# Second SwiGLU block: feature pairs without the norm's factor, and two direct tiles in place of four

## The chip, the cores and the metric

The kernel runs on one core of one Trainium2 chip. A core has engines that each work through their own list of instructions: TensorE (PE, matrix products), VectorE (DVE), ScalarE (ACT), GpSimd (POOL) and SyncE (SP, which here only issues transfers). They wait for one another by semaphores. The metric is the device time of one execution in microseconds (us), from start to end.

## The reference

One decoder layer, float32, on x of 512 tokens by 1024 features:

```python
x = x + 0.5 * swiglu(rms_norm(x, g_ffn1), w_ffn1_gate, w_ffn1_up, w_ffn1_down)
h = rms_norm(x, g_mix)
# three groups of heads (windowed attention, convolution, cross-attention to 256 memory tokens)
x = x + concat(y_attn, y_conv, y_mem) @ w_out
x = x + 0.5 * swiglu(rms_norm(x, g_ffn2), w_ffn2_gate, w_ffn2_up, w_ffn2_down)

def swiglu(x, w_gate, w_up, w_down):
    return (jax.nn.silu(x @ w_gate) * (x @ w_up)) @ w_down

def rms_norm(x, g):
    return x * lax.rsqrt(jnp.mean(x * x, axis=-1, keepdims=True) + EPS) * g
```

The hidden width is 2816, 22 tiles of 128. The two SwiGLU blocks have the same shapes; the change is in the second.

## The kernel before

x lies transposed: 8 feature tiles of 128 partitions by 512 tokens (`x[:, d]`). Every float32 operand is split in a high part, rounded to the type that PE multiplies (`whi`, `xh`, `hh`, `bh`), and the rest (`wlo`, `xl`, `hl`, `bl`), and a product is three matmuls: high x high, high x rest, rest x high. ACT makes the high part (line 167 for weights), DVE the rest (line 168).

**The norm's factor.** The gain is multiplied into `xh` and `xl` (`scaled_split`, lines 358 and 359). The factor of a token, `rb`, is a number for each token and so commutes with the product over features. It is made late: the squares of all feature tiles are summed (`sqsum`, line 373), `Norm.stats` sums them over partitions on PE (line 378) and takes the reciprocal root on DVE in small steps (lines 332 to 337), then broadcasts it (line 383); `Norm.spread` transposes that on PE (`tp<-ident,t`, line 391) and copies it to `rb` (line 392).

**The tiles of a SwiGLU block.** A tile f of the hidden width is made in one of two ways.

- *Direct* (f < `N_DIRECT` = 4): `mm3` multiplies gate and up by `xh` and `xl`, 24 matmuls of 512 columns each (lines 347 to 349). `evac` multiplies both results by `rb` (lines 410 and 413), with the silu on ACT and their product on DVE (line 414).
- *Fast* (the others): gate and up over two halves of the features, and x over two halves of the features and of the tokens, are a 2 x 2 by 2 x 2 block product with seven block products in place of eight (`fast` and `product`, lines 444 to 446), 12 matmuls of 256 columns each, 84 in all. It needs sums of weights (`make_sums`, lines 126 to 129: `s` of four 512-column adds) and combinations of x. `blocks(k)` makes the latter for the feature tiles k and k + 4, with the factor `rb` in them, one k after each direct tile: `braw` (21, 22, 11, 12; line 423, twice), `bmade` (T3, Q1, Q2, T4; lines 432 to 434) and their split `bh`, `bl` (seven blocks of 256; lines 436 and 437).

The T4 product of tile f takes a weight split of its own (`vhi`, `vlo`, 512 columns, one buffer each) and writes to a bank of the tag `sc`; the other products write to `mm` banks, of which there are four.

**The down product** runs in six rounds over hidden tiles 0-3, 4-7, 8-11, 12-15, 16-17 and 18-21 (`ROUNDS`); `steps(f)` says which pieces stand within which tile: the first three pieces of round 0 ahead of tile 4, the fourth in tile 5, then one in each tile from 8. A round's result is scaled by 0.5 and added to x: on DVE (line 506), but for the first two pieces of round 0 by ACT (line 502) and an accumulating transfer of POOL (line 503). The result is stored as the last round makes it.

**What sets the order.** Transfers of weights are issued on SP ahead of use (`W.load_to`), splits three items ahead (`W.next`). Within that a scheduler fixes each engine's list when the program is built; numbers in the names below follow the order in which the code was written, so that the rows show how far an engine's list leaves it. Each tag of a pool has a number of buffers (`sum` 3, `kept` 3, `t` 5, `mm` 4, `sc` and `tp` 2), and a new tile waits for the buffer's last reader.

## Time and profile before

| | us |
|---|---|
| three runs | 869.84, 865.34, 865.73 |
| median | 865.73 |
| profiled execution, its own time | 870.17 |
| span of the profile, first to last instruction | 868.1 |
| PE busy in it | 861.3 |
| DVE busy | 698.3 |
| ACT busy | 446.0 |
| POOL busy | 27.9 |

The profiled execution is near the slowest of the three runs, and 2.07 us of its time lie outside the span. A row of the timeline gives the start, the duration, engine, line, operation, the output and the inputs by name; in brackets stands how long the engine was idle before it and which instruction it waited for. In the order of time the second block takes: tiles 0 and 1 from 529.20 to 551.16, tiles 2 and 3 to 573.14, the first pieces of the down product to 589.94, the fast tiles from there to the last product at 864.9.

### The profile page before, as it was taken

How to read it: one execution, taken by the hardware profiler on the slowest of the kernel's cores; microseconds unless marked ns; L12 is line 12 of the kernel's file. 1: busy time of each engine (PE TensorE's matmuls, PEld its weight loads, DVE VectorE, ACT ScalarE, POOL GpSimd, SP SyncE). 2: the span in 40 equal slices, each digit the busy share in tenths (PEclk: the TensorE clock that was granted, in tenths of full speed). 3: DMA queues.
4: the chain of work that ended last, by engine and by line, in shares of the span. 5: the costliest groups of instructions: out<-in, count | busy, mean ns of one | idle time of the engine just before them, and what ended most of it. 6: DMA issues, size and time to landing. Idle time of an engine off the chain costs nothing.

```text
span 868.1 us, 15720 instructions
## 1 busy us (share of the span) xinstructions
PE 861.3 (99%) x6361; PEld 795.1 (92%) x6361; DVE 698.3 (80%) x1163; ACT 446.0 (51%) x740; POOL 27.9 (3%) x30
## 2 busy tenths in 40 slices
PE   9999999999999999999999999999999999999998
PEld 5889999999999999988776878889999999999998
DVE  7998877777868887869989976997987878787772
ACT  7455545455554454632939754454554444545440
POOL 0010000000000000300000021010000000000000
PEclk9999999999999999999999999999999999999999
DMA  7326334334454344232020333336333333333312
GB/s 271 122 83 165 94 97 122 99 110 134 111 145 146 97 113 130 95 97 62 0 62 13 110 89 84 99 90 159 105 106 121 95 121 85 116 98 99 121 49 99
DMA packets 34809, 91.45 MB, mean 105 GB/s; under 512 B 3248, under 2 KB 5808, under 8 KB 34736
## 3 DMA queue, kind: packets, MB, share of 16 engines
q1 hardware_dynamic: 32000, 85.99, 32.1%
q0 software_dynamic: 1584, 2.88, 2.1%
q10 hardware_dynamic: 1152, 1.57, 0.7%
q8 instruction: 50, 0.82, 0.4%
q14 instruction: 23, 0.19, 0.1%
HBM read 85.45 MB, written 2.10 MB: 101 GB/s over the span
## 4 chain that ended last, share of the span: by engine, by line
PE 92%; DVE 3%; ACT 2%; issue 1%; DMA 1%; SPq 0%; ACTq 0%; DVEq 0%
PE mm L347 15%; PE mm L348 14%; PE mm L349 14%; PE mm L444 11%; PE mm L446 11%; PE mm L445 11%; PE sc L444 2%; PE sc L446 2%; PE sc L445 2%; PE sc L347 1%; PE sc L349 1%; PE sc L348 1%; PE tp L948 1%; PE tp L962 1%; ACT p L913 1%
## 5 line engine op out<-in xcount | busy, mean ns | idle before, releaser
L444 PE MATMUL mm<-bh,whi 128*128 128x256 f32 x864 | 239.9, 278 | 0.2 <-ACT kept L459 0.2
L446 PE MATMUL mm<-bh,wlo 128*128 128x256 f32 x864 | 239.6, 277 | 0.0
L445 PE MATMUL mm<-bl,whi 128*128 128x256 f32 x864 | 239.6, 277 | 0.0
L348 PE MATMUL mm<-hl,whi 128*128 128x256 f32 (+1 forms) x640 | 184.7, 289 | 0.0
L349 PE MATMUL mm<-hh,wlo 128*128 128x256 f32 (+1 forms) x640 | 184.6, 289 | 0.0
L347 PE MATMUL mm<-hh,whi 128*128 128x256 f32 (+1 forms) x640 | 184.1, 289 | 0.0
L167 ACT CAST whi<-wraw 128x1024 fp32r<-128x1024 f32 (+2 forms) x122 | 124.1, 1021 | 106.2 <-PE mm L348 45.0
L168 DVE TENSOR_TENSOR wlo<-wraw,whi 128x1024 fp32r<-128x1024 f32 (+2 forms) x122 | 145.4, 1193 | 34.4 <-ACT whi L167 34.0
L446 PEld LDWEIGHTS mm<-bh,wlo 128*128 128x128 f32 x864 | 163.1, 189 | 0.0
L444 PEld LDWEIGHTS mm<-bh,whi 128*128 128x128 f32 x864 | 162.2, 188 | 0.5 <-ACT kept L459 0.4
L445 PEld LDWEIGHTS mm<-bl,whi 128*128 128x128 f32 x864 | 162.2, 188 | 0.2
L349 PEld LDWEIGHTS mm<-hh,wlo 128*128 128x128 f32 x640 | 120.8, 189 | 2.9
L347 PEld LDWEIGHTS mm<-hh,whi 128*128 128x128 f32 x640 | 120.1, 188 | 2.7
L348 PEld LDWEIGHTS mm<-hl,whi 128*128 128x128 f32 x640 | 120.1, 188 | 2.7
L168 DVE TENSOR_TENSOR wlo<-s,whi 128x1024 fp32r<-128x1024 f32 x72 | 87.9, 1222 | 36.0 <-ACT whi L167 35.6
L167 ACT CAST whi<-s 128x1024 fp32r<-128x1024 f32 x72 | 75.5, 1050 | 47.3 <-PE mm L445 43.5
L348 PE MATMUL mm<-xl,whi 128*128 128x512 f32 x192 | 75.9, 395 | 0.6 <-DVE xl L359 0.5
L347 PE MATMUL mm<-xh,whi 128*128 128x512 f32 x192 | 76.3, 402 | 0.0
L349 PE MATMUL mm<-xh,wlo 128*128 128x512 f32 x192 | 75.8, 395 | 0.0
L506 DVE SCALAR_TENSOR_TENSOR x<-mm,x 128x512 f32<-128x512 f32 x80 | 54.0, 682 | 3.7 <-PE mm L349 3.7
L167 ACT CAST vhi<-wraw 128x512 fp32r<-128x512 f32 x36 | 22.4, 622 | 62.7 <-PE sc L445 48.5
L126 DVE TENSOR_TENSOR s<-wraw 128x512 f32<-128x512 f32 x36 | 24.9, 691 | 32.6 <-DMA wraw<-in_wgu 32.6
(243 smaller groups left out, 1368.3 us busy)
## 6 DMA issues: line engine op xcount, KB each, us to landing
wraw<-in_wgu SPq DMA_DIRECT2D x86, 512.0 KB, 3.6
wraw<-in_wd SPq DMA_DIRECT2D x44, 512.0 KB, 3.7
wraw<-in_win SPq DMA_DIRECT2D x12, 512.0 KB, 3.5
x<-t POOLq DMA_DIRECT2D x8, 256.0 KB, 6.1
out<-t SPq DMA_DIRECT2D x7, 256.0 KB, 2.0
x<-in_xT SPq DMA_DIRECT2D x3, 512.0 KB, 6.6
wraw<-in_wout_a SPq DMA_DIRECT2D x6, 256.0 KB, 2.7
wraw<-in_wgu SPq DMA_DIRECT2D x4, 256.0 KB, 4.9
```

Source lines behind the costliest of these rows:

```text
L126: nc.vector.tensor_tensor(s12[:, l], u[:, l], u[:, r], op=ALU.add)
L167: nc.scalar.copy(hi[:, :cols], raw[:, :cols])
L168: nc.vector.tensor_tensor(lo[:, :cols], raw[:, :cols], hi[:, :cols].bitcast(F32), op=ALU.subtract)
L347: PE.matmul(ps[:, t], wh[:, w], hi(k)[:, t], start=one, stop=False, skip_group_check=cut > 1)
L348: PE.matmul(ps[:, t], wh[:, w], lo(k)[:, t], start=False, stop=False, skip_group_check=cut > 1)
L349: PE.matmul(ps[:, t], wl[:, w], hi(k)[:, t], start=False, stop=end, skip_group_check=cut > 1)
L444: PE.matmul(ps, wh[:, c], bh[k][:, block], start=one, stop=False, skip_group_check=not first)
L445: PE.matmul(ps, wh[:, c], bl[k][:, block], start=False, stop=False, skip_group_check=not first)
L446: PE.matmul(ps, wl[:, c], bh[k][:, block], start=False, stop=end, skip_group_check=not first)
L506: DVE.scalar_tensor_tensor(o, ps, 0.5, xd, op0=ALU.mult, op1=ALU.add)
L913: ACT.activation(self.p[n, h][:, c], src[h][:, i, c], AF.Exp, scale=self.fac[:, m : m + 1], bias=self.neg[:, m : m + 1], accum_out=self.de ...
L948: PE.transpose(ps[:, i * P : (i + 1) * P], self.p[n, h][:, c : c + P], ident)
```

## The change

In the second block only (`last` is true there, and `memory` is false):

- `N_DIRECT` becomes (4, 2): tiles 2 and 3 are fast, too.
- The two halves of the features are now the even and the odd feature tiles, not the first and the last four (`halves(..., near)`), so that a pair of blocks needs two neighbouring feature tiles.
- `pairs(k)` takes the place of `blocks(k)`: it leaves `rb` out (`braw` is ACT's x times gain), makes only T3, Q1, Q2 and T4, and stands ahead of tile 0 for all four k. The blocks 11, 21 and 22 are slices of `xh` and `xl` (`block_of`).
- Since `rb` is left out of the blocks, a fast tile multiplies its gate and its up result by `rb` on DVE.
- Round 0 of the down product adds to x on DVE alone.
- Hidden tiles, and the mixed heads' `yh` and `yl`, are allotted in other pools and at other times.

```diff
-N_DIRECT = 4
+N_DIRECT = (4, 2)
...
+    def halves(w, near):
+
+        return [w.rearrange("p (k h m) -> p h k m" if near else "p (h k m) -> p h k m", h=2, k=4)[:, h] for h in range(2)]
+
+    def make_sums(self, i, near):
...
+        (gl, gr), (ul, ur) = (self.halves(self.raw[j], near) for j in (i, i + 1))
...
+        (s1, s2), (s4, s3) = (self.halves(s, False) for s in (s12, s43))
+        nc.vector.tensor_tensor(s1, ul, ur, op=ALU.add)
+        nc.vector.tensor_tensor(s2, gl, s1, op=ALU.add)
+        nc.vector.tensor_tensor(s4, gr, s2, op=ALU.add)
+        nc.vector.tensor_tensor(s3, gl, ul, op=ALU.add)
...
+        n_direct = N_DIRECT[last]
+
+        def htile(f, name):
+
+            if last and f % 8 > 1:
+                return pool.tile([P, T], F32R, tag="hid", name=nm(name), bufs=12)
+            return atile(name)
...
+        def pairs(k):
+
+            raw = pool.tile([P, 4, 256], F32, tag="sum", name=nm("braw"), bufs=SUM_BUFS)
+            made = pool.tile([P, 4, 256], F32, tag="sum", name=nm("bmade"), bufs=SUM_BUFS)
+            for i, d in enumerate((2 * k + 1, 2 * k)):
+                ACT.activation(raw[:, 2 * i : 2 * i + 2].rearrange("p a b -> p (a b)"), x[:, d], AF.Identity,
+                               scale=par[:, gain + d : gain + d + 1])
+            b21, b22, b11, b12 = (raw[:, i] for i in range(4))
+            bh[k] = pool.tile([P, 4, 256], F32R, tag="bh", name=nm("bh"), bufs=4)
+            bl[k] = pool.tile([P, 4, 256], F32R, tag="bl", name=nm("bl"), bufs=4)
+            DVE.tensor_tensor(made[:, B_T3 : B_Q1 + 1], raw[:, 1:3], raw[:, 3:4].to_broadcast([P, 2, 256]), op=ALU.subtract)
+            DVE.scalar_tensor_tensor(made[:, B_Q2], made[:, B_T3], -1.0, b11, op0=ALU.mult, op1=ALU.subtract)
+            DVE.tensor_tensor(made[:, B_T4], b21, made[:, B_Q2], op=ALU.add)
+            ACT.copy(bh[k], made)
+            DVE.tensor_tensor(bl[k], made, bh[k].bitcast(F32), op=ALU.subtract)
+
+        def block_of(k, block):
+
+            if not last or block <= B_T4:
+                return bh[k][:, block], bl[k][:, block]
+            d = 2 * k + (block != B_11)
+            t = slice(256, 512) if block == B_22 else slice(0, 256)
+            return xh[d][:, t], xl[d][:, t]
...
+                o = 2 * k * P + woff // 4 if last and block in (B_11, B_21) else woff + k * P
...
             DVE.tensor_tensor(g, de, s12, op=ALU.add)
+            if last:
+                DVE.tensor_tensor(g, g, rb, op=ALU.mult)
             ACT.activation(g, g, AF.Silu)
...
+            if last:
+                DVE.tensor_tensor(u, u, rb, op=ALU.mult)
             DVE.tensor_tensor(u, u, g, op=ALU.mult)
...
-                    if r == 0 and g < 2:
+                    if r == 0 and g < 2 and not last:
...
+        if last:
+            for k in range(4):
+                pairs(k)
...
-            if f >= N_DIRECT:
+            if f >= n_direct:
                 fast(f, mid)
...
-                        blocks(0)
+                        if not last:
+                            blocks(0)
...
-                    blocks(f)
...
+                    if not last:
+                        blocks(f)
...
     def put_y(i, src):
...
+        yh[i], yl[i] = (
+            atile(n) if i < spare else mix.tile([P, T], F32R, name=f"{n}{i}") for n in ("yh", "yl")
+        )
```

What moves, on DVE and on PE. Line numbers of the changed kernel are higher (179 for 168, 384 for 373, 370 for 359, 391 for 380, 394 for 383, 402 for 391, 403 for 392, 428 for 410, 489 to 491 for 444 to 446).

DVE before, from the last weight split that both orders share (`wlo_5934`, called `wlo_5935` afterwards) to the root's steps: sums of squares, `xl` of the last feature tile, then the statistics of the norm (`s_6081<-tp_6076`).

```order
L168 TENSOR_TENSOR wlo_5934<-wraw_5786,whi_5933 128x1024
L373 TENSOR_TENSOR sqsum_5856<-sqsum_5856,t_6003 128x512
L359 SCALAR_TENSOR_TENSOR xl_6007<-x,par,xh_6006 128x512
L380 TENSOR_SCALAR s_6081<-tp_6076 128x4
L168 TENSOR_TENSOR wlo_6023<-wraw_5937,whi_6022 128x1024
L332 TENSOR_SCALAR rtok<-s_6081 128x4
L333 TENSOR_SCALAR s_6083<-s_6081 128x4
L168 TENSOR_TENSOR wlo_6101<-wraw_5976,whi_6100 128x1024
```

DVE afterwards, from the same split (467 to 469 are a pair's T3 with Q1, Q2 and T4, 471 its `bl`):

```order
L179 TENSOR_TENSOR wlo_5935<-wraw_5783,whi_5934 128x1024
L467 TENSOR_TENSOR bmade_6016<-braw_6015 128x512
L384 TENSOR_TENSOR sqsum_5857<-sqsum_5857,t_6004 128x512
L370 SCALAR_TENSOR_TENSOR xl_6008<-x,par,xh_6007 128x512
L468 SCALAR_TENSOR_TENSOR bmade_6016<-bmade_6016,braw_6015 128x256
L469 TENSOR_TENSOR bmade_6016<-braw_6015,bmade_6016 128x256
L179 TENSOR_TENSOR vlo_6246<-wraw_5977,vhi_6245 128x512
L467 TENSOR_TENSOR bmade_6027<-braw_6026 128x512
L471 TENSOR_TENSOR bl_6020<-bmade_6016,bh_6019 128x1024
L468 SCALAR_TENSOR_TENSOR bmade_6027<-bmade_6027,braw_6026 128x256
L469 TENSOR_TENSOR bmade_6027<-braw_6026,bmade_6027 128x256
L467 TENSOR_TENSOR bmade_6038<-braw_6037 128x512
```

Two rows stood between that split and the statistics' first row before; now fifteen do: beside the same two, steps of the first three pairs, the split of tile 2's T4 weights (`vlo_6246`) and one more weight split.

DVE before, the end of the root, the broadcast (383), the copy of `rb` (392), and the first multiply of `evac` (410), which frees a bank of tile 0:

```order
L335 TENSOR_TENSOR s_6084<-rtok 128x4
L336 TENSOR_TENSOR s_6084<-s_6084,s_6083 128x4
L337 SCALAR_TENSOR_TENSOR rtok<-s_6084,rtok 128x4
L383 COPY t_6096<-rtok 128x512
L392 COPY rb<-tp_6130 128x512
L168 TENSOR_TENSOR wlo_6161<-wraw_6020,whi_6160 128x1024
L410 TENSOR_TENSOR t_6136<-mm_6014,rb 128x512
```

DVE afterwards, from the same step on (133 to 136 are sums of weights, now for tiles 2 and 3):

```order
L133 TENSOR_TENSOR s_100_6306<-wraw_6074 128x512
L347 TENSOR_TENSOR s_6132<-s_6132,s_6131 128x4
L136 TENSOR_TENSOR s_100_6307<-wraw_6068,wraw_6074 128x512
L348 SCALAR_TENSOR_TENSOR rtok<-s_6132,rtok 128x4
L179 TENSOR_TENSOR wlo_6275<-wraw_6068,whi_6274 128x1024
L394 COPY t_6144<-rtok 128x512
L134 TENSOR_TENSOR s_100_6306<-wraw_6068,s_100_6306 128x512
L179 TENSOR_TENSOR vlo_6377<-wraw_6074,vhi_6376 128x512
L403 COPY rb<-tp_6184 128x512
L135 TENSOR_TENSOR s_100_6307<-wraw_6068,s_100_6306 128x512
L428 TENSOR_TENSOR t_6190<-mm_6062,rb 128x512
```

The root's small steps stood in one piece; now a sum or a split for the fast tiles stands between each two of them, as well as between the broadcast, the copy and the first multiply.

PE before, around the transposes of the norm's factor (`tp_6130`), which stand between the gate product of tile 1 (`mm_6098`) and its up product (`mm_6099`):

```order
L349 MATMUL mm_6098<-xh_6006,wlo_5973 128x512
L391 MATMUL tp_6130<-ident,t_6096 128x128 x4
L347 MATMUL mm_6099<-xh_5858,whi_6016 128x512
L348 MATMUL mm_6099<-xl_5859,whi_6016 128x512
L349 MATMUL mm_6099<-xh_5858,wlo_6017 128x512
```

PE afterwards, behind the up product of tile 1: the T4 product of tile 2 (`sc_6240`, its last row is the first here) and that of tile 3 (`sc_6371`), with the transposes in it (`tp_6184`):

```order
L491 MATMUL sc_6240<-bh_6052,vlo_6246 128x256
L489 MATMUL sc_6371<-bh_6019,vhi_6376 128x256
L490 MATMUL sc_6371<-bl_6020,vhi_6376 128x256
L402 MATMUL tp_6184<-ident,t_6144 128x128 x4
L491 MATMUL sc_6371<-bh_6019,vlo_6377 128x256
L489 MATMUL sc_6371<-bh_6030,vhi_6376 128x256
```

and where tile 3's T4 product ends and tile 2's first product into an `mm` bank (`mm_6238`) begins:

```order
L490 MATMUL sc_6371<-bl_6053,vhi_6376 128x256
L491 MATMUL sc_6371<-bh_6052,vlo_6377 128x256
L489 MATMUL mm_6238<-xh_5859,whi_6070 128x256
L490 MATMUL mm_6238<-xl_5860,whi_6070 128x256
L491 MATMUL mm_6238<-xh_5859,wlo_6071 128x256
```

The transposes have moved from the middle of tile 1 to a place behind it, and two T4 products stand ahead of the rest of tile 2.

47 lines of the change are left out of this document (24 added, 23 removed).

## The prediction

> **What bounds the kernel now.** I read the page's busy times and chain first, then the table of windows for the stages of the second block, then the rows of TensorE (PE), VectorE (DVE) and ScalarE (ACT) around the place where that block starts.
>
> ```profile
> span 868.1 us, 15720 instructions
> PE 861.3 (99%) x6361; PEld 795.1 (92%) x6361; DVE 698.3 (80%) x1163; ACT 446.0 (51%) x740; POOL 27.9 (3%) x30
> PE 92%; DVE 3%; ACT 2%; issue 1%; DMA 1%; SPq 0%; ACTq 0%; DVEq 0%
> ```
>
> PE is busy 99% of the span and is 92% of the chain. So a change can shorten the kernel only by giving PE less to do, and lengthen it only by more work there or by a wait of PE.
>
> The windows (time range, length, then busy us and count of each engine, granted clock, DMA):
>
> ```profile
> core 0: us, PE busy (x) PEld busy (x) DVE busy (x) ACT busy (x) POOL busy (x), PEclk, DMA share, GB/s
> 125.00:265.00 140.00, 140.00 (x1191) 140.00 (x1190) 105.44 (x140) 71.12 (x112) 2.58 (x3) 1.00 0.41 118
> 280.00:350.00 70.00, 70.00 (x620) 70.00 (x619) 59.24 (x97) 33.27 (x48) 0.18 (x2) 1.00 0.38 112
> 551.16:573.14 21.98, 21.98 (x97) 18.03 (x96) 21.80 (x33) 12.14 (x16) 0.00 (x0) 1.00 0.28 85
> 573.14:589.95 16.81, 16.81 (x74) 13.54 (x73) 16.23 (x23) 7.98 (x12) 3.48 (x4) 1.00 0.47 106
> 640.00:700.00 60.00, 60.00 (x532) 60.00 (x531) 46.04 (x60) 29.25 (x46) 0.00 (x0) 1.00 0.37 110
> 700.00:820.00 120.00, 120.00 (x1061) 120.00 (x1061) 92.78 (x121) 58.99 (x90) 0.00 (x0) 1.00 0.35 106
> ```
>
> 551.16 to 573.14 is the two direct tiles that become fast: 96 matmuls of 512 columns (the 97th only touches the edge), 21.98/96 = 0.229 us each. 640 to 700 is fast work of 256 columns: 60/532 = 0.1128 us each. The reader should also see DVE at 21.80 of 21.98 and 16.23 of 16.81: here PE's cover is thin. And 125 to 265 runs at 140/1191 = 0.1176 us, 4.1% slower per matmul than 280 to 350 (0.1129), at the same granted clock; that matters for a rival below.
>
> **The change part by part.** *PE's own work.* A direct tile is 48 matmuls, 48 x 0.229 = 10.99 us; a fast one is 7 products of 12, 84 x 0.1128 = 9.47 us. Two tiles: 21.98 - 18.95 = **-3.03 us**. The blocks 11, 22 and 21 now come as slices of xh and xl, at the same 256 columns; the stream price is taken as the same. Nearest rows either side are 0.1128 and 0.1145 (= 0.229/2, the price per 256 columns that xh and xl have today); the upper one on the 3 x 12 x 2 = 72 matmuls of these blocks in the two tiles is +0.1 us, on all 720 of the 20 fast tiles +1.2 us. I take nothing.
>
> The Trainium skill, "TensorE: Matmul & The Clock Gate", section "Back-to-back issue gap", gives N/2.4 + 2.5 ns for a lone warm matmul. By it a 512-column matmul is 215.8 ns and a 256-column one 109.2 ns, an estimate of 2 x (10.36 - 9.17) = 2.4 us saved instead of 3.03, and a forecast 0.6 us higher; the trace's 229 and 112.8 ns differ and decide.
>
> *The norm's way to PE.* Here the time goes back. The factor rb comes from DVE: eps, nine small steps of the reciprocal root, a broadcast to 512 columns, then four transposes on PE and a copy. Before, DVE stood idle ahead of it and PE did not wait:
>
> ```profile
> 531.21 1.21 DVE L168 TENSOR_TENSOR wlo<-wraw,whi 128x1024 fp32r<-128x1024 f32 x1
> 539.80 0.16 DVE L380 TENSOR_SCALAR s<-tp 128x4 f32<-128x4 f32 x1 [6.11 <-PE tp L378]
> 541.09 0.17 DVE L333 TENSOR_SCALAR s<-s 128x4 f32<-128x4 f32 x1
> 541.16 1.22 DVE L168 TENSOR_TENSOR wlo<-wraw,whi 128x1024 fp32r<-128x1024 f32 x1
> 542.30 0.16 DVE L335 TENSOR_TENSOR s<-rtok 128x4 f32<-128x4 f32 x1
> 542.49 0.16 DVE L336 TENSOR_TENSOR s<-s,s 128x4 f32<-128x4 f32 x1
> 544.07 0.43 DVE L383 COPY t<-rtok 128x512 f32<-128x512 f32 x1
> 545.85 0.69 DVE L392 COPY rb<-tp 128x512 f32<-128x512 f32 x1 [1.36 <-PE tp L391]
> 546.46 1.22 DVE L168 TENSOR_TENSOR wlo<-wraw,whi 128x1024 fp32r<-128x1024 f32 x1
> 554.66 0.74 DVE L423 SCALAR_TENSOR_TENSOR braw<-x,par,rb 128x512 f32<-128x512 f32 x1
> 555.32 1.22 DVE L437 TENSOR_TENSOR bl<-bmade,bh 128x1024 fp32r<-128x1024 f32 x1
> 559.46 0.68 DVE L432 TENSOR_TENSOR bmade<-braw 128x512 f32<-128x512 f32 x1
> 560.06 0.95 DVE L436 TENSOR_TENSOR bl<-braw,bh 128x768 fp32r<-128x768 f32 x1
> 560.93 0.41 DVE L433 SCALAR_TENSOR_TENSOR bmade<-bmade,braw 128x256 f32<-128x256 f32 x1
> 561.26 1.21 DVE L168 TENSOR_TENSOR wlo<-wraw,whi 128x1024 fp32r<-128x1024 f32 x1
> ```
>
> From start to start these rows give DVE's prices: 1024 columns 1.14 us (541.16 to 542.30), 512 columns 0.60 (559.46 to 560.06), 256 columns 0.33 (560.93), a 512-column scalar_tensor_tensor 0.66 (554.66), a small step 0.07 when nothing hangs on it (541.09) and 0.19 when it does (542.30), the broadcast 0.43 as its own time.
>
> In the changed kernel the same wlo is the last common DVE row, so I start at 531.21. From there to the end of the broadcast the new order has nine 1024-column steps (10.26 us: four bl of the pairs and five weight splits), twelve of 512 (7.20: four bmade, sqsum, one vlo, six sums of weights), one xl (0.66), eight of 256 (2.68), twelve small ones (0.96 at 0.08, since something else stands between most of them), the broadcast (0.43): 22.2 us. Add 0.65 for the third pair, whose raw data reuse one of three sum buffers and wait for the first pair's bl and then for two ACT steps,
>
> ```profile
> 515.78 0.71 ACT L358 ACTIVATE xh<-x,par 128x512 fp32r<-128x512 f32 x1
> 516.39 0.62 ACT L369 ACTIVATE t<-x 128x512 f32<-128x512 f32 x1
> ```
>
> 0.61 us each, of which two 256-column steps of DVE cover 0.67, and about 0.3 for gaps: 23.1, so the broadcast ends at 554.35 instead of 544.5. The 6.11 us of idle that DVE had is used up.
>
> ```profile
> 545.22 0.60 PE L391 MATMUL tp<-ident,t 128*128 128x128 f32 x4
> 545.57 0.48 PE L347 MATMUL mm<-xh,whi 128*128 128x512 f32 x1
> 551.16 0.39 PE L347 MATMUL sc<-xh,whi 128*128 128x512 f32 x1
> 573.14 0.39 PE L347 MATMUL mm<-hh,whi 128*128 128x512 f32 x1
> ```
>
> PE now ends tile 1 at 551.16 - 0.35 = 550.81 (the transposes have moved behind it). It has two T4 products brought forward, which need no factor and no mm bank: 24 x 0.1128 = 2.71, and the transposes, 0.35. Unhindered it would reach tile 2's first own product at 553.87. That product needs one of four mm banks, all held by g and u of tiles 0 and 1, and the first is free when DVE has multiplied g of tile 0 by rb. DVE's row after the broadcast: a sum (0.60), vlo of tile 3 (0.60), then the copy of rb (0.61), a sum (0.60), the multiply (0.68): 554.35 + 3.09 = 557.45. **PE idle 3.58 us**, in pieces: some 0.65 for the second vhi/vlo (one buffer, freed by the first T4 product), some 1.5 for the broadcast, 0.8 for vlo of tile 3, 0.7 for the bank. Both ends: with every small step at the dependent 0.19 the broadcast is 12 x 0.11 = 1.3 later, 4.9 us; without the 0.65, the 0.3 and half of a sum it is 1.3 earlier, 2.3 us. I take 3.58 because the new order interleaves the chain as rows 541.09 to 541.16 are interleaved today.
>
> Then 168 - 24 = 144 matmuls are left, 16.24 us: the first down product starts at 557.45 + 16.24 = 573.69 instead of 573.14, **+0.55**.
>
> *Evacuation of the first down round.* Four accumulating transfers on POOL and four ACT scalings go, four DVE adds come:
>
> ```profile
> L506 DVE SCALAR_TENSOR_TENSOR x<-mm,x 128x512 f32<-128x512 f32 x80 | 54.0, 682 | 3.7 <-PE mm L349 3.7
> L503 POOL DMA_DIRECT2D x<-t x8 | 7.1, 898 | 116.5 <-DVE bl L437 114.8 <-ACT t L502 1.7
> L502 ACT ACTIVATE t<-mm 128x512 f32<-128x512 f32 x8 | 4.8, 600 | 4.3 <-PE mm L349 4.3
> L475 DVE TENSOR_TENSOR t<-kept,mm 128x512 f32<-128x512 f32 x36 | 24.6, 682 | 5.7 <-PE mm L446 4.7 <-ACT kept L473 0.7
> ```
>
> DVE gains 4 x 0.68 = 2.7 us there, but the four blocks of 2 x 0.66 + 0.60 + 0.33 + 0.33 + 0.87 + 1.14 = 4.6 us each have left for pairs of 0.60 + 0.33 + 0.33 + 1.14 = 2.4 each, already done. Nothing on the path; SP's queue has the same 178 rows in the same order and POOL's only loses.
>
> *Two multiplies by rb in each fast tile.* 0.68 us each by L475, a two-operand row from PSUM or SBUF. From 700 to 820 about eight tiles run (84 + 48 matmuls, 14.9 us): DVE goes from 92.78 to 92.8 + 16.1 x 0.68 = 103.8 of 120, 86%. The cover is the 16 us left. The rearranged weight sums (four strips in place of one flat half) are taken at the flat price, since L475, which runs over two halves, takes the same 0.682. Nothing on the path, but slack shrinks (rival C).
>
> *The end.* The last tile's hidden data come later, between its T3 and the down step that uses them:
>
> ```profile
> 839.25 0.69 DVE L475 TENSOR_TENSOR t<-kept,mm 128x512 f32<-128x512 f32 x1 [2.10 <-PE mm L446]
> 839.98 0.69 DVE L479 TENSOR_TENSOR t<-t,t 128x512 f32<-128x512 f32 x1
> ```
>
> In the new order DVE has from that subtraction on: 0.73, the multiply by rb 0.61, a weight split 1.14, the product 0.61, two adds of 0.66, hl 0.68, ready at 839.25 + 5.09 = 844.34. PE ends T3 there at about 839.2 and has three down steps of 12 matmuls ahead (36 x 0.1128 = 4.06) and then ten more until hl is read (1.13): 844.39. No wait, or a few hundredths; I take 0.05.
>
> The sum: -3.03 + 3.58 + 0.05 = **+0.6 us**, on the profiled execution 870.17 + 0.6 = 870.8. That execution is at the high end (runs 865.34, 865.73, 869.84), so on the median: 865.73 + 0.6 = **866.3**.
>
> **The rivals.** *B, the stall doesn't come.* If the scheduler's order meets the transposes early enough, or the chain slips through as before, PE loses nothing and the whole -3.03 shows: 862.7. For it: 1.36 us of idle ahead of the copy at 545.85 were hidden before. Against: 22.2 us of DVE rows stand ahead of the broadcast and PE has 19.9 of cover (531.21 to 551.16).
>
> *C, the slower side: the slow stream.* It follows one short stall of PE in a fast stage:
>
> ```profile
> 119.29 0.28 PE L446 MATMUL mm<-bh,wlo 128*128 128x256 f32 x1
> 119.73 0.39 PE L444 MATMUL mm<-bh,whi 128*128 128x256 f32 x1 [0.17 <-ACT kept L459]
> ```
>
> After that 0.17 us wait on ACT's evacuation each matmul is 4.1% longer until about 276, some 157 us, 6.4 us in all. With DVE at 86% a late evacuation in tiles 4 to 21 could do the same. A stretch that long gives 866.3 + 6.4 = 872.7; from 590 to 864 without end, 274 x 0.041 = 11.2, 877.5. It decides (over 0.5% slower, 4.33 us, less the 0.6) from 3.7/0.041 = 90 us of slow stream. Against: DVE was at 59.24 of 70 (85%) from 280 to 350 and the stream ran at 0.1129.
>
> *D, PE slows after its pause.* The rows of the start are the only ones where PE is seen slower:
>
> ```profile
> L302 PE MATMUL tp<-warm 128*128 128x512 bf16 x11 | 4.9, 632 | 1.2 <-DVE pair L315 1.2
> ```
>
> 4.9/11 = 0.44 us against 0.229: if the pause brings that back for as long, PE loses (0.44 - 0.229) x 11 = 2.4 us, 868.7. Against: the clock reads 1.00 in each window, and the pauses are separate, 1.5 us at most. The Trainium skill, same page, section "HAM oscillation — how this bites in real kernels", wants no idle gap over about 3.4 us; by that rule D doesn't happen here unless the four pauses merge into one.
>
> **How the numbers follow.** The forecast (865.0 to 867.6 by the bounds of the pause) 0.50; B 0.22; C 0.17; D 0.08; others 0.03. The range of 8 in 10 runs from B's 862.7, just below it, to 871.0 (a part of C, and D on top of the long pause): 862.6 to 871.0. 0.5%, 861.4 and 870.1, is about what a measurement of this kernel can tell from no change: faster 0.05 (B with a shorter stream, and others), slower 0.20 (C, and a little of D), same 0.75.
>
> **What would show it.** Right: PE idle of 2.3 to 4.9 us between 550 and 558, released by DVE's broadcast, vlo and the multiply; first down product near 573.7; DVE at about 104 of 120 late; 0.1128 per matmul with xh operands. Wrong: first down product near 570 (B); 0.1176 anywhere after 590 (C); matmuls of over 0.2 us at 256 columns after 557 (D); a weight split late for PE, which no row here shows.

## The result, and the profile after

The changed kernel is slower: 876.83 us median of 19 runs (872.02 to 887.31) against 866.92 us of the kernel before (863.86 to 872.75, 19 runs), ratio 1.0113, 95% interval [1.0085, 1.0141]. A ratio leaves out single runs more than 1.5% above the fastest of their kernel (887.31 here, 882.36 and 880.38 below), and isn't the quotient of the medians, which are of all runs. The forecast was +0.6 us, the measured difference of the medians +9.9.

The profiled execution of the changed kernel took 873.94 us, 3.77 more than that of before. First the page of it: span and instructions, busy times, the chain by engine.

```profile
span 872.1 us, 15902 instructions
PE 861.9 (99%) x6433; PEld 798.0 (91%) x6433; DVE 722.4 (83%) x1207; ACT 446.2 (51%) x752; POOL 24.4 (3%) x26
PE 87%; DVE 7%; issue 2%; ACT 2%; DMA 2%; SPq 0%; DVEq 0%; ACTq 0%
```

PE is busy as long as before, though it has 3 us less of products to make, and its share of the chain fell from 92% to 87% while DVE's rose from 3% to 7%. Next the windows (start:end and length, busy us and count per engine, granted clock behind POOL):

```profile
125.00:265.00 140.00, 140.00 (x1238) 140.00 (x1237) 108.46 (x146) 73.44 (x116) 2.59 (x3) 1.00 0.41 119
544.46:551.87 7.41, 5.07 (x30) 4.35 (x28) 7.41 (x15) 2.09 (x3) 0.00 (x0) 0.79 0.41 137
545.40:548.81 3.41, 1.54 (x12) 1.11 (x10) 3.41 (x9) 0.69 (x2) 0.00 (x0) 1.00 0.28 110
548.81:552.23 3.42, 2.95 (x14) 2.67 (x13) 3.42 (x7) 0.63 (x1) 0.00 (x0) 0.50 0.43 120
551.87:569.06 17.19, 17.19 (x146) 16.98 (x146) 14.95 (x21) 11.12 (x20) 0.00 (x0) 0.99 0.31 108
640.00:700.00 60.00, 60.00 (x529) 59.93 (x529) 50.56 (x69) 27.66 (x44) 0.00 (x0) 1.00 0.34 105
740.00:860.00 120.00, 120.00 (x1021) 120.00 (x1020) 91.12 (x122) 50.24 (x77) 0.00 (x0) 1.00 0.30 93
```

Four readings. In the first block this execution ran at 140/1238 = 0.1131 us, where the profiled execution of before ran at 0.1176: tile 1 of the second block is done at 544.46 instead of 550.81 (551.16 less the transposes that now stand behind it), and the first block's code is the same in both. From there to tile 2's own products PE has 7.41 us, busy for 5.07. The products of tiles 2 and 3 run to 569.06, where the first down product starts. And from 740 on a matmul takes 120/1021 = 0.1175 us, where 640 to 700 has 0.1134 and before had 0.1131 from 700 to 820.

So the difference of the two spans, +4.0, is made of -6.35 (the first block), then 569.06 - 544.46 = 24.60 us against 573.14 - 550.81 = 22.33 (**+2.3 at the front**), then 299.7 us from the first down product to the last one against 291.6 (**+8.1 in the rest of the block**). The waits of PE from tile 1's end on (line, releaser; us in total, times, longest) show where it begins; before, the same view from 529 to the end has no row at all:

```profile
PE tp L402 <- DVE t L394: 1.3, 1, 1.3
PE mm L489 <- ACT kept L504: 1.2, 2, 0.9
PE sc L489 <- ACT vhi L178: 0.6, 1, 0.6
PE sc L491 <- DVE vlo L179: 0.5, 1, 0.5
```

The front, on PE and on DVE (the timeline: start, duration, engine, line, operation, and the wait):

```profile
544.46 0.28 PE L489 MATMUL sc<-bh,vhi 128*128 128x256 f32 x1
...
546.59 0.39 PE L489 MATMUL sc<-bh,vhi 128*128 128x256 f32 x1 [0.59 <-ACT vhi L178]
...
548.36 0.73 PE L402 MATMUL tp<-ident,t 128*128 128x128 f32 x4 [1.28 <-DVE t L394]
549.57 0.58 PE L491 MATMUL sc<-bh,vlo 128*128 128x256 f32 x1 [0.47 <-DVE vlo L179]
549.95 0.42 PE L489 MATMUL sc<-bh,vhi 128*128 128x256 f32 x1
550.16 0.41 PE L490 MATMUL sc<-bl,vhi 128*128 128x256 f32 x1
```

```profile
524.97 1.21 DVE L179 TENSOR_TENSOR wlo<-wraw,whi 128x1024 fp32r<-128x1024 f32 x1
547.89 0.42 DVE L394 COPY t<-rtok 128x512 f32<-128x512 f32 x1
```

DVE's list came out as costed: from the common split to the end of the broadcast 548.31 - 524.97 = 23.3 us (forecast 23.1). PE waits 0.59, 1.28 and 0.47, 2.34 in all. The granted clock is at half from 548.81 to 552.23, behind the first two of these waits: in the 3.41 us ahead of it PE was busy for 1.54 and idle for 1.87. While it lasts, a matmul of 256 columns takes 0.21 us (549.95 to 550.16) instead of 0.113.

In the rest of the block, tile 7, which has the longest wait. First DVE's chain to u: the subtraction (L522), the new multiply (L527), the product (L528).

```profile
632.37 0.68 DVE L522 TENSOR_TENSOR t<-kept,mm 128x512 f32<-128x512 f32 x1
632.97 0.69 DVE L179 TENSOR_TENSOR vlo<-wraw,vhi 128x512 fp32r<-128x512 f32 x1
633.57 0.69 DVE L527 TENSOR_TENSOR t<-t,rb 128x512 f32<-128x512 f32 x1
634.17 1.22 DVE L179 TENSOR_TENSOR wlo<-wraw,whi 128x1024 fp32r<-128x1024 f32 x1
635.31 0.69 DVE L528 TENSOR_TENSOR t<-t,t 128x512 f32<-128x512 f32 x1
```

Then ACT's list, in the same tile before the change (two rows) and after it (two rows), and PE after it:

```profile
636.40 0.62 ACT L402 CAST hh<-t 128x512 fp32r<-128x512 f32 x1 [0.79 <-DVE t L479]
636.93 1.04 ACT L167 CAST whi<-wraw 128x1024 fp32r<-128x1024 f32 x1
```

```profile
636.03 0.62 ACT L420 CAST hh<-t 128x512 fp32r<-128x512 f32 x1 [1.66 <-DVE t L528]
636.56 0.38 ACT L504 ACTIVATE kept<-mm 128x256 f32<-128x256 f32 x1
```

```profile
636.99 0.39 PE L489 MATMUL mm<-xh,whi 128*128 128x256 f32 x1 [0.91 <-ACT kept L504]
...
725.84 0.28 PE L491 MATMUL mm<-bh,wlo 128*128 128x256 f32 x1
726.02 0.39 PE L489 MATMUL mm<-bh,whi 128*128 128x256 f32 x1
726.25 0.28 PE L490 MATMUL mm<-bl,whi 128*128 128x256 f32 x1
726.37 0.28 PE L491 MATMUL mm<-bh,wlo 128*128 128x256 f32 x1
```

ACT's cast hh stands at the head of its list and waits 1.66 us for u; the copy to kept that lets PE write the same bank again stands behind it; PE waits 0.91. Two things have changed here. From the end of the subtraction to the end of the product the chain takes 2.46 us in 16 of tiles 4 to 21 and 2.94 in the other two, where before it took 0.73 and 1.20 in as many. The 1.73 us are the new multiply (0.60) and a weight split (1.14), which in the new order stands between it and the product. And what follows hh in ACT's list was a weight cast in all 18 tiles; now it is a copy to kept in 16 of them.

The row at 726.02 is a smaller kind of delay: no wait is booked, but the matmul starts 0.07 late and takes 0.23 to the next. From it to the end each matmul takes 0.1178 instead of 0.1133.

### The profile page after: what moved, and what is told of

It is laid out like the page before. It is cut to its first block, busy times and chain, and to the rows that moved or that the text cites. A ratio compares the mean times of both kernels' runs of the same rounds, so it can differ in the third digit from the quotient of the medians.

```text
span 872.1 us, 15902 instructions
## 1 busy us (share of the span) xinstructions
PE 861.9 (99%) x6433; PEld 798.0 (91%) x6433; DVE 722.4 (83%) x1207; ACT 446.2 (51%) x752; POOL 24.4 (3%) x26
## 4 chain that ended last, share of the span: by engine, by line
PE 87%; DVE 7%; issue 2%; ACT 2%; DMA 2%; SPq 0%; DVEq 0%; ACTq 0%
PE mm L358 14%; PE mm L359 14%; PE mm L360 14%; PE mm L489 11%; PE mm L490 11%; PE mm L491 11%; PE sc L491 2%; DVE wlo L179 2%; PE sc L490 2%; PE sc L489 2%; PE tp L1003 1%; DMA wraw<-in_wgu 1%; PE sc L358 1%; PE sc L360 1%; PE sc L359 1%
## 5 line engine op out<-in xcount | busy, mean ns | idle before, releaser
L489 PE MATMUL mm<-bh,whi 128*128 128x256 f32 x672 | 186.8, 278 | 0.0
L490 PE MATMUL mm<-bl,whi 128*128 128x256 f32 x672 | 186.0, 277 | 0.0
L491 PE MATMUL mm<-bh,wlo 128*128 128x256 f32 x672 | 186.0, 277 | 0.0
L178 ACT CAST whi<-wraw 128x1024 fp32r<-128x1024 f32 (+2 forms) x120 | 122.1, 1021 | 93.5 <-PE mm L359 38.5
L489 PEld LDWEIGHTS mm<-bh,whi 128*128 128x128 f32 x672 | 126.1, 188 | 0.6
L491 PEld LDWEIGHTS mm<-bh,wlo 128*128 128x128 f32 x672 | 126.6, 188 | 0.0
L490 PEld LDWEIGHTS mm<-bl,whi 128*128 128x128 f32 x672 | 126.2, 188 | 0.1
L512 ACT ACTIVATE t<-t 128x512 f32<-128x512 f32 x38 | 24.0, 633 | 96.1 <-DVE t L511 67.6
L358 PE MATMUL mm<-xh,whi 128*128 128x512 f32 x176 | 69.9, 402 | 0.0
L489 PE MATMUL mm<-xh,whi 128*128 128x256 f32 x240 | 67.2, 280 | 1.3 <-ACT kept L504 1.2
L490 PE MATMUL mm<-xl,whi 128*128 128x256 f32 x240 | 66.8, 278 | 0.0
```

What stands on the lines that cost most here:

```text
L178: nc.scalar.copy(h, raw)
L358: PE.matmul(ps[:, t], wh[:, w], hi(k)[:, t], start=one, stop=False, skip_group_check=cut > 1)
L489: PE.matmul(ps, wh[:, c], hi, start=one, stop=False, skip_group_check=not first)
L490: PE.matmul(ps, wh[:, c], lo, start=False, stop=False, skip_group_check=not first)
L491: PE.matmul(ps, wl[:, c], hi, start=False, stop=end, skip_group_check=not first)
L512: ACT.activation(g, g, AF.Silu)
```

## The experiments

Two theories were set up after the result, and others against them. A (late cast): the waits after 590 come from u's longer chain, through ACT's list. E (draw): each restart of PE within a stretch of 256-column matmuls draws one of two rates and keeps it. Against A stand B (DVE's total load), C (the front) and D (the operands); against E stands F (the slow rate belongs to what the change brings). These letters are not those of the prediction's rivals.

**Without the multiply on u.**

```diff
-            if last:
-                DVE.tensor_tensor(u, u, rb, op=ALU.mult)
```

> The changed kernel without the multiply of a fast tile's up result by rb (the output leaves that factor out of u). Theory A (late cast): the multiply lengthens the DVE chain that ends in u, the cast hh waits for it at the head of ACT's list, the copies to kept stand behind it, and PE waits for those; after such waits the stream of matmuls drops to 0.118 us. Then without it PE has no wait on kept after 590 and runs at 0.1133 to the end: the waits (2.9 us) and the slow stream (5.6 us) go, about +1 us against the kernel before instead of +9.4. Theory B (load): it is DVE's total work that counts, half of the added work is left, about +5. Theory C (front): the pause and the cold clock where tile 2 starts make the difference, +9 as before. Theory D (operands): slices of xh and the strided weight sums make the stream slow, +9.

877.04 median of 10 (867.39 to 882.36), ratio 1.0094 [1.0060, 1.0128]. The times fall in groups: 867.4, 867.7, 868.6; six from 874.1 to 877.7; one at 882.4. The profiled one (877.25) has, from 545 to the end, only the front's three waits of PE, and yet:

```profile
600.00:860.00 260.00, 260.00 (x2186) 258.93 (x2186) 201.95 (x266) 121.49 (x184) 0.00 (x0) 1.00 0.33 100
```

260/2186 = 0.1189 us, a few 512-column matmuls included. The kernel before has 2271 in the same window, 0.1145: here it is the slow rate all through. A is right on the waits: the chain to u takes 0.73 to 0.80 us again in 16 of tiles 4 to 21, and a weight cast follows hh there. It is wrong that this brings the rate back: the rate is slow from a late start at 574.40 on, within the first down products. B, with half of the added load left, expected waits. D expected the slow rate, but the same operands also gave the three times near 868.

**The factor on the gate path.**

```diff
             ACT.activation(g, g, AF.Silu)
+            if last:
+                DVE.tensor_tensor(g, g, rb, op=ALU.mult)
...
-                DVE.tensor_tensor(u, u, rb, op=ALU.mult)
```

> The changed kernel with the second multiply by rb moved from u to the gate path, after the silu, where it runs before the last product of the tile is done; the result is the same and DVE has as many instructions as in the changed kernel. Theory A (late cast): the chain that ends in u is as short as before, no wait on kept, 0.1133 to the end, +1 to +2 us against the kernel before. Theory B (load): DVE's work is that of the changed kernel, +9. Theories C (front) and D (operands): +9.

873.20 median of 6 (868.83 to 879.96), ratio 1.0084 [1.0039, 1.0130]: three at 868.8 to 870.2, three from 876.2. The profiled one (876.31) changes its rate twice after 590:

```profile
640.00:695.00 55.00, 55.00 (x488) 55.00 (x487) 44.99 (x63) 24.22 (x38) 0.00 (x0) 1.00 0.33 97
705.00:860.00 155.00, 155.00 (x1318) 155.00 (x1318) 121.84 (x164) 68.17 (x104) 0.00 (x0) 1.00 0.32 94
```

55/488 = 0.1127 between 640 and 695, 155/1318 = 0.1176 from 705, and 0.1178 between 600 and 635 by the starts of single matmuls. The changes stand at its only wait on kept (0.18 us at 638.7) and at one matmul at 697.34 that takes 0.19 to the next instead of 0.11. With as many DVE instructions as the changed kernel it has one wait there instead of two and a series of late starts, which is for A and against B. The test isn't as clean as was expected: in 14 of tiles 4 to 21 the product ends 1.74 us behind the subtraction, for a weight split still stands between them, and a copy to kept still follows hh. And a restart can bring the rate back as well as take it.

**Four direct tiles, all else of the change.**

```diff
-N_DIRECT = (4, 2)
+N_DIRECT = (4, 4)
```

> The changed kernel with four direct tiles in the second block, as before; pairs, multiplies by rb and xh slices stay. Theory A (late cast): 18 of 20 fast tiles keep their waits and the slow stream can come, +4 to +9 us against the kernel before. Theory C (front): the pause and the cold clock go, and PE has the 3 us more of direct work, between 0 and +3, with PE at 0.1133 after 590. Theories B (load) and D (operands): like A, +6 to +12, but without waits on kept under D.

875.74 median of 4 (875.40 to 883.26), ratio 1.0143 [1.0100, 1.0185]. PE waits 1.5 us for the broadcast at the front, the clock reads 1.00, and after 590 there are seven waits on kept of 2.7 us in all. C alone is out: beside 3 us more of direct work some 7 us are left, and they aren't at the front.

**Without both multiplies.**

```diff
-            if last:
-                DVE.tensor_tensor(g, g, rb, op=ALU.mult)
...
-            if last:
-                DVE.tensor_tensor(u, u, rb, op=ALU.mult)
```

> The changed kernel without both multiplies by rb in the fast tiles (the output leaves the factor out of them). Theory A (late cast): as without the one on u, +1 us against the kernel before, no wait on kept after 590, 0.1133. Theory B (load): all added work is gone, 0 to +1 and clearly less than without the one on u alone. Theories C (front) and D (operands): still +9.

869.27 median of 8 (867.04 to 878.68), ratio 1.0058 [1.0025, 1.0091]; six of the eight at 867.0 to 870.3. No wait after the front's three, and 2271 matmuls from 600 to 860, exactly as before the change. So D is out, with the changed kernel's operands. This is the front with little else: in the profile 24.70 us from tile 1's end to the first down product where before had 22.33, and 291.9 from there to the last one where before had 291.6; the median is 3.7 above.

**The kernel before with one wait added,** in tile 9, where ACT makes a copy to kept twelve times.

```diff
             ACT.copy(s12[:, l], b)
+            for _ in range(11 if last and f == 9 else 0):
+                ACT.copy(s12[:, l], b)
```

> The kernel before the change, with one thing added: in fast tile 9 of the second block ACT makes the first copy to kept twelve times instead of once, so that PE waits there once, for some 0.5 to 1 us, near 655 to 665. Nothing else differs from the kernel before. Theory E (draw): each restart of PE within a stretch of 256-column matmuls draws one of two rates, 0.1133 or 0.1178 us, and keeps it until the next restart. Then the executions fall in two groups, some at +1 us against the kernel before and some at +8 to +10 (205 us x 0.04 more). Theory F: the slow rate belongs to what the change brings (operands, more work on DVE); then all executions lie within +0.5 to +1.5 and the stream stays at 0.1133.

874.42 median of 9, ratio 1.0080 [1.0046, 1.0114]: one at 867.05, one at 871.01, seven from 873.7 to 880.4. The profiled execution happens to be the lowest:

```profile
649.76 0.39 PE L444 MATMUL mm<-bh,whi 128*128 128x256 f32 x1 [0.78 <-ACT kept L461]
```

```profile
700.00:860.00 160.00, 160.00 (x1414) 160.00 (x1413) 114.03 (x149) 69.04 (x103) 0.00 (x0) 1.00 0.31 96
```

One wait of 0.78 us, 160/1414 = 0.1132 after it, and 867.05. The other eight have the same instructions and are 4 to 13 us longer; the groups that E forecast are there, F's single one isn't. That those eight run at the slow rate after tile 9 is inferred from their times: only one execution is profiled.

**The same wait in tile 20.**

```diff
-            for _ in range(11 if last and f == 9 else 0):
+            for _ in range(11 if last and f == 20 else 0):
```

> As the kernel with one stall in tile 9, but with the eleven more copies in tile 20, so that PE waits once near 825 to 830 with some 38 us of 256-column matmuls left. Theory E (a restart draws the rate and keeps it to the next one): the slow group lies only 38 x 0.04 = 1.5 us above the fast one, so all executions are within +0.5 to +3 of the kernel before's own two groups. If instead a stall itself cost some 8 us wherever it stands: +7 to +9 in most executions, as with tile 9.

868.36 median of 9: seven from 867.15 to 869.06, two at 874.7 and 875.2 (the kernel before has such a second group of its own: 6 of its 25 runs beside these are at 871.2 to 872.4, the others at 864.0 to 867.9). Ratio 1.0026 [0.9993, 1.0059]. The profiled one (867.87) shows the draw itself, before and behind the wait:

```profile
740.00:810.00 70.00, 70.00 (x620) 70.00 (x619) 55.04 (x73) 33.92 (x53) 0.00 (x0) 1.00 0.35 105
816.00:860.00 44.00, 44.00 (x376) 44.00 (x375) 23.20 (x31) 12.30 (x18) 0.00 (x0) 1.00 0.20 67
```

```profile
813.35 0.38 PE L444 MATMUL mm<-bh,whi 128*128 128x256 f32 x1 [0.30 <-ACT kept L461]
```

70/620 = 0.1129, then 44/376 = 0.1170, where the kernel before has 391 matmuls in the same 44 us. With nothing of the change in it the kernel slows down behind a wait of 0.30 us, and stays slow for the 50 us that are left: some 2 us. The wait in tile 9, with 215 us behind it, left seven of nine executions 8 us or more above the median of before. So it is a rate that lasts, and not a price of the wait.

**The two multiplies alone,** put into the kernel before.

```diff
             DVE.tensor_tensor(g, de, s12, op=ALU.add)
+            if last:
+                DVE.tensor_tensor(g, g, rb, op=ALU.mult)
...
+            if last:
+                DVE.tensor_tensor(u, u, rb, op=ALU.mult)
             DVE.tensor_tensor(u, u, g, op=ALU.mult)
```

> The kernel before the change, with nothing of it but the two multiplies by rb in each fast tile of the second block (so that factor enters twice there); four direct tiles, blocks and front as before. Theory A+E (late cast, then draws): PE gets waits on kept after 590 in about half of the fast tiles, 2 to 3 us in all, and in most executions a slow stretch: +3 to +11 against the kernel before, without any pause at the front. Theory C (the front is the loss): 0 to +1. Theory B (load): waits that grow along the block, spread over DVE and ACT.

874.73 median of 6 (873.41 to 878.67), ratio 1.0093 [1.0064, 1.0122]: +8.1 us from two instructions per tile, with no pause at the front. The waits from 535 on, and the windows before and behind the last of them:

```profile
PE mm L444 <- ACT kept L455: 1.5, 2, 0.8
PE mm L444 <- ACT kept L459: 0.8, 1, 0.8
```

```profile
690.00:735.00 45.00, 45.00 (x397) 44.91 (x396) 36.83 (x51) 20.05 (x33) 0.00 (x0) 1.00 0.36 106
770.00:860.00 90.00, 90.00 (x765) 89.96 (x765) 66.65 (x90) 35.37 (x55) 0.00 (x0) 1.00 0.31 92
```

Three waits, 2.3 us, all on the copies to kept; 45/397 = 0.1134 ahead, 90/765 = 0.1176 behind. The chain to u is that of the changed kernel (2.46 us in 16 tiles, 2.94 in two), so the weight split comes between with the multiply. As A and E expected; C is out as the main loss.

**The cast hh on DVE** in the changed kernel.

```diff
-            ACT.copy(h_hi[f], t)
+            DVE.tensor_copy(h_hi[f], t) if last and f >= n_direct else ACT.copy(h_hi[f], t)
```

> The changed kernel with the cast hh of a fast tile on DVE instead of ACT: it can no longer stand ahead of the copies to kept in ACT's list, while DVE gets 0.6 us more per tile. Theory A (late cast at the head of ACT's list): no wait of PE on kept after 590. Theory B (DVE's load): more and longer waits than in the changed kernel, over 3 us in all. The rate after 590 is drawn at the last restart (theory E), so the time alone says little: 866 with 0.1133, 877 with 0.1178.

Two executions, 874.8 and 879.8. From 646 to the end, where the changed kernel has a late start in four tiles, there is one of 0.07 us at 853, with 0.6 us more work on DVE per tile (the rate, drawn slow at 642, stays slow). Before that two waits remain:

```profile
PE mm L359 <- DVE hl L421: 1.2, 1, 1.2
PE mm L489 <- ACT kept L500: 0.6, 1, 0.6
```

So A holds for the tiles with down products, and B's growing waits don't come; in tiles 6 and 7, which have none (9.5 us each), another wait takes their place.

**The root on POOL, the transposes in the middle of tile 1's up product.**

```diff
-                    norm.stats()
+                    norm.stats(POOL if last else None)
...
+                    if half:
+                        uh, ul = W.next()
+                        mm3(u, uh, ul, range(4), xhk, xlk, True, False)
                     if f == 1:
                         norm.spread()
...
+                    if half:
+                        mm3(u, uh, ul, range(4, 8), xhk, xlk, False, True)
```

> The changed kernel with the nine steps of the norm's reciprocal root on POOL (idle there) instead of DVE, and the transposes of the factor in the middle of tile 1's up product; the result is the same. The broadcast then waits for no weight sums or pairs between the steps. Theory A+E with the front as costed: the broadcast ends some 6 us earlier, PE's pause at tile 2 falls from 2.3 us to under 1, no cold clock, first down product 3 to 4 us earlier; the waits on kept after 590 stay, with their draws: 866 to 876. If the pause is bound by something else (weight splits), it stays over 1.5 us.

877.16 median of 3, ratio 1.0146 [1.0086, 1.0207]. The nine steps run on POOL; the diff leaves out how `rsqrt` is told to. The transposes hardly wait (0.26 us late), but the pause moved and grew, and the clock went to half:

```profile
546.00:550.13 4.13, 0.43 (x5) 0.25 (x3) 4.13 (x6) 2.05 (x3) 0.00 (x0) 0.85 0.80 243
550.13:554.50 4.37, 4.37 (x20) 4.37 (x21) 3.89 (x6) 2.10 (x4) 0.00 (x0) 0.50 0.03 9
```

PE waits 3.70 us for the first multiply that frees a bank, with DVE busy in all 4.13 us of that window. What bounds the front is all that stands in DVE's list ahead of that multiply, not the root's steps; the expectation was wrong.

**The same, with the gate's second multiply on POOL.**

```diff
             ACT.activation(g, g, AF.Silu)
+            if last:
+                POOL.tensor_tensor(g, g, rb, op=ALU.mult)
...
-                DVE.tensor_tensor(u, u, rb, op=ALU.mult)
```

> The former, and the second multiply by rb moved from u to the gate path, on POOL; the result is the same. DVE's chain to u is as short as before the change and DVE loses one 512-column step per tile. Theory A+E: no wait on kept after 590, hence nothing that draws the slow rate there: 860 to 863 in most executions, 2 to 4 us less than the kernel before. If waits remain (POOL's multiply late for u), 870 and more.

883.70 median of 4, ratio 1.0222 [1.0168, 1.0276], where 860 to 863 was expected: eight waits on kept of 5.8 us in all. A multiply on POOL takes 1.40 us, and u waits for it in two tiles, 2.1 us in all; where the other six waits come from was not followed up.

**Two of the four weight sums of a fast tile on POOL, the gate's multiply on DVE** (as above; `near` is true in the second block).

```diff
+        E = nc.gpsimd if near else nc.vector
...
-        nc.vector.tensor_tensor(s4, gr, s2, op=ALU.add)
-        nc.vector.tensor_tensor(s3, gl, ul, op=ALU.add)
+        E.tensor_tensor(s4, gr, s2, op=ALU.add)
+        E.tensor_tensor(s3, gl, ul, op=ALU.add)
```

> The changed kernel with two of the four weight sums of each fast tile of the second block on POOL (1.47 us each there) and the multiply by rb of u moved to the gate path on DVE; the result is the same. DVE has 1.2 us less per tile. By the rows of the changed kernel the broadcast ends 3 us earlier, the pause at tile 2 falls from 2.3 us in three pieces to about 1.6 in two, and tile 2's own products start 2.5 us earlier. Theory A+E: no wait on kept after 590, so mostly 0.1133: 862 to 866, with a second group 8 to 11 higher where the restart at tile 2 drew the slow rate. If POOL's sums come late, waits on the casts of weights appear.

892.17 median of 4, ratio 1.0274 [1.0224, 1.0324]. PE waits 4.2 us for the broadcast and 10.1 us on kept, where 862 to 866 and no such wait was expected.

**All four of them on POOL,** on top of the former.

```diff
-        nc.vector.tensor_tensor(s1, ul, ur, op=ALU.add)
-        nc.vector.tensor_tensor(s2, gl, s1, op=ALU.add)
+        E.tensor_tensor(s1, ul, ur, op=ALU.add)
+        E.tensor_tensor(s2, gl, s1, op=ALU.add)
```

> As the former, but all four weight sums of a fast tile on POOL, 5.9 us per tile of 14.9; the result is the same. DVE's rows ahead of the broadcast are 4.8 us fewer. If the front is bound by DVE's work: pause under 1 us, and 861 to 864 in the fast group. If POOL's chain of four sums (two of them in sequence ahead of the second split) is late there: a pause of 1.5 to 3 us at the transposes, released by DVE behind a weight split, and 864 to 868.

881.83 median of 3, ratio 1.0164 [1.0125, 1.0204]. From 651 to the end there isn't a single wait and the rate holds (200/1767 = 0.1132 from 660 to 860), but the front waits 7.4 us for the broadcast and the first down step 3.9.

**All four sums of tile 3 and of tiles 8 to 21 on POOL,** those of the others on DVE again.

```diff
-        E = nc.gpsimd if near else nc.vector
+        E = nc.gpsimd if pool else nc.vector
...
-                W.add_pair(flat(gu[f, 0]), flat(gu[f, 1]), [down(*d) for d in mid], not memory)
+                W.add_pair(flat(gu[f, 0]), flat(gu[f, 1]), [down(*d) for d in mid], not memory, not memory and (f == 3 or f > 7))
```

> The changed kernel with the four weight sums of tile 3 and of tiles 8 to 21 on POOL, those of tiles 2 and 4 to 7 on DVE, and the second multiply by rb of a fast tile moved from u to the gate path on DVE; the result is the same. DVE has 2.4 us less ahead of the first multiply that frees a bank, and 2.4 us less per tile from tile 8. Theory A+E: no wait on kept from tile 8 on, at most one or two before it; at the front the pause falls to 1 to 2 us and the cold clock may go. Then the lower group of executions is at 862 to 865, and a higher group, where a restart before tile 8 drew the slow rate for the rest, 8 to 11 above it. If POOL's sums for tile 3 come late: a wait on a weight split there, 867 and more.

883.21 median of 6, ratio 1.0180 [1.0146, 1.0214], with a wait of 5.2 us for the broadcast, where 1 to 2 were expected. Why is in DVE's rows and POOL's:

```profile
552.60 0.16 DVE L347 TENSOR_TENSOR s<-rtok 128x4 f32<-128x4 f32 x1
...
555.62 1.26 DVE L349 SCALAR_TENSOR_TENSOR rtok<-s,rtok 128x4 f32<-128x4 f32 x1
```

```profile
554.65 2.21 POOL L134 TENSOR_TENSOR s<-wraw 128x512 f32<-128x512 f32 x1 [20.39 <-DVE wlo L180]
```

While POOL adds, DVE's four-element steps take 1.1 to 1.3 us instead of 0.16 and end when POOL's instruction does: 556.88 and 556.86 in these rows. So here work moved to POOL wasn't simply taken off DVE.

**Three direct tiles and the gate's multiply on DVE** (as above).

```diff
-N_DIRECT = (4, 2)
+N_DIRECT = (4, 3)
```

> The changed kernel with three direct tiles instead of two, and the second multiply by rb of a fast tile moved from u to the gate path on DVE; the result is the same. PE gets 1.5 us more work than in the changed kernel and the transposes stand in tile 2's gate product, when by the rows DVE has just made the broadcast. Theory A+E with the front bound by DVE's list: pause under 0.5 us and no cold clock; few waits on kept: 862 to 864 in the lower group, 8 to 11 more where a restart drew the slow rate. If the front's loss does not depend on PE's cover: a pause of 1 to 3 us stays.

876.45 median of 10 (871.28 to 879.54), ratio 1.0097 [1.0065, 1.0130]. The clock stays at 1.00; a wait of 1.3 us for the broadcast stays (PE reached the transposes at 545.8, the broadcast was done at 547.06), and 0.5 for the first down step. After that no wait is booked, but a start 0.24 late at 636 and smaller ones draw the rate: it is 0.1178 from 585 to 635 and again from 665 on.

**The same, with hh of tiles 8 to 21 on DVE.**

```diff
-            ACT.copy(h_hi[f], t)
+            DVE.tensor_copy(h_hi[f], t) if last and f > 7 else ACT.copy(h_hi[f], t)
```

> The former, and the cast hh of tiles 8 to 21 on DVE, where it cannot stand ahead of ACT's copies to kept; the result is the same. Theory A+E: no wait on kept from tile 8 on, so no draws there; 862 to 864 in most executions unless the rate was drawn slow before tile 8. If DVE's load (0.6 us more per tile) matters: waits on weight splits or on hl, and 866 or more.

873.43 median of 10 (870.07 to 878.85), ratio 1.0083 [1.0053, 1.0113]. Beside the wait for the broadcast (1.3 us) there is one on kept, before tile 8 (1.2), and one on a weight split (0.3, at 745.4), and behind the latter the slow rate. The products that were saved don't show: 1.5 us less work, and 2.8 us of waits. No version here is faster than the kernel before.

## Why the prediction was wrong

**The step that failed** is the one on the two multiplies: "Nothing on the path, but slack shrinks". It weighed DVE's load (86%) and didn't ask what is queued behind the instruction that waits for u. It is the cast hh on ACT, and behind it now stand the copies to kept, for which PE waits. It also took the order of the lists as it was: for the last tile the prediction counts the multiply and a weight split between subtraction and product, for the others neither, and u came 1.73 us later in all of tiles 4 to 21. That the two multiplies bring the waits is shown by the multiplies alone (+8.1 us, three waits, all on kept); that it is their place and not the load, by the kernel without the multiply on u (no wait after the front, with half of the added load) and by hh on DVE (none from tile 8 on, with more load). How the 1.73 us share the blame is only half shown: with the split in the chain but not the multiply (the factor on the gate path) a wait of 0.18 us and late starts were left, and no run has the multiply without the split.

**Rival C had the mechanism and its price, at a chance of 0.17.** A stretch like the one after 119.73 was said to cost 6.4 us, and 11 at most; in the profile it is (868.8 - 726) x 0.0045/0.1178 = 5.5. With some 2.7 us for the waits and late starts, counted from start to start, these are the 8.1 of that part. What was wrong is the argument against it. That DVE was at 85% from 280 to 350 without a slow stream said nothing, since it isn't load that sets it off but a late start of PE, whatever makes it; and from 590 on the changed kernel makes seven of them where there was none. That a restart draws the rate is shown by the two kernels with one added wait; why it does, and which rate it draws, isn't.

**The front** was costed at +0.55 and measured +2.3. DVE's sum was right (23.3 us for 23.1). Tile 2's first own product came 7.41 us behind tile 1's end, where 2.71 for the T4 products and 0.35 for the transposes were costed: 4.35 late and not 3.58, 0.77 more and inside the stated 2.3 to 4.9. Of the 4.35 the waits are 2.34. The sum had no term for the rest: ten matmuls at half clock, from 549.57 to 551.87, took 2.30 us instead of 1.13, and the transposes and the starts behind the waits took some 0.8. The 144 matmuls that follow took 17.19 us and not 16.24, 0.95 more: the end of the half clock, two late starts, and the slow rate from 559.17 to 567.41. 0.55 + 0.77 + 0.95 is the +2.3. Rival D had the half clock, with 2.4 us and 0.08. Its argument against, that the pauses are separate and 1.5 us at most, fell: two, the longest 1.28, were enough. By the Trainium skill, "TensorE: Matmul & The Clock Gate", section "HAM oscillation — how this bites in real kernels", the rule is no idle gap of PE over about 3.4 us; here the measurement decides, and it differs.

**What was right**: PE's own prices (0.1134 per matmul from 640 to 700, xh slices included; the rearranged sums 0.684 us as the flat ones), DVE's load to within 5 us (99.18 of 120 from 700 to 820, forecast 103.8, before 92.78), the removed accumulating transfers (nothing on the path), and no sign of a later end.

The saved products are in the trace (84 matmuls at 0.1134 in place of 48 at 0.229), but no version showed their 3.03 us as time: in each of them something waited.

## What to carry to other kernels

An instruction added to a chain is priced at the engine that waits for the chain's end: look there at what stands behind the waiting instruction in the same list, and who waits for that. Read the new order of the lists for it, too: here one added multiply brought a weight split along that took twice its time. Where PE is at 99% and has no wait in the trace, the first wait can cost many times its length (one added wait of 0.78 us moved the median by 8.9), so a change that saves 0.3% of PE's work has to be free of new ones. And before work is moved to an idle engine, look in the trace at what the busy one does while the idle one runs.

## What the runs showed of the hardware

- A stream of 256-column matmuls has two rates, 0.1133 and 0.1178 us, at a granted clock of 1.00 in both. In the second block, in the profiles of all these runs, it changes only where PE's even spacing breaks, by as little as 0.05 us (0.16 to the next at 664.69 with three direct tiles), in either direction, and then lasts: 143 us in the changed kernel, over 250 us without the multiply on u. Not every late start changes it. The two groups of the kernel before, some 6.5 us apart, fit it: its profiled execution, at 870.17, ran slow from 119.73 to 276.
- The granted clock went to half by the sum of PE's idle time, and not by the longest wait. Between two changes of it in one profile there always lies a whole number of stretches of 3.41 us. In the second block, in all runs, a stretch at full clock in which PE idled 1.82 us or more was followed by one at half clock (1.82 with the factor on the gate path, 1.87 in the changed kernel, each in two waits), and one with 1.80 us or less was not (1.71, a single wait, with all four sums on POOL; 1.46 with four direct tiles).
- DVE instructions of 0.16 us took 1.1 to 1.3 us while POOL ran a 512-column add of 1.3 to 2.2 us. By the Trainium skill, "GPSIMD Engine Reference", section "1. Specifications", the two engines share their access to SBUF, with contention for DVE instructions in a 2-port mode or with two SBUF inputs: the row at 555.62 agrees, a step with both inputs there, and so does the subtraction `t<-kept,mm` of the same run, which reads one of its inputs from PSUM and stays at 0.67 to 0.69 us in all 13 tiles in which POOL runs beside it.
